# An encoder block's last stage: one run's weight sums made earlier, output rows read early and written in place, the last row tile in two parts

## The chip, the cores and the metric

The kernel runs on 1 core of one Trainium2 chip. The metric is the device time of one execution in microseconds (us). Three executions of the kernel before took 805.09, 804.85 and 802.40 us, median 804.85 us. The execution that was profiled took 804.06 us.

## The reference

One layer of an encoder: 512 positions, width 1024, all inputs in float32.

```python
h = h + rms_norm(mix_out, norm_mix_post)           # gated MLP and attention branches ahead of this
n2 = rms_norm(h, norm_mlp_pre)
hid = jnp.square(jax.nn.relu(einsum('bsd,df->bsf', n2, w_up)))   # 4096 hidden columns
mlp_out = einsum('bsf,fd->bsd', hid, w_down)                     # 512 x 4096 times 4096 x 1024
h = h + rms_norm(mlp_out, norm_mlp_post)                         # the output
```

Everything in this document happens in the last two lines, the down projection, its norm and the sum with `h` (which the kernel keeps in device memory as `h2d`).

## The kernel before, in words

Float32 products are made from three passes: each operand is split into a high part (ACT copies it into a narrower format, line 79) and the rest (DVE subtracts, line 80), and TensorE (PE) adds high*high, high*rest and rest*high (lines 1041, 1042 and 1043). So no matmul of a block can start before ACT and DVE have split it.

The output of the down projection is four row tiles of 128 rows by two halves of 512 columns, in eight banks of PSUM. `X` are the banks of rows 0 and 1 in the left half, `W` rows 0 and 1 in the right half, `Y` rows 2 and 3 in the left half, `Z` rows 2 and 3 in the right half. 32 tiles of 128 hidden columns are to be summed. The first 8 go in plainly (`plain`, four calls of two tiles). The other 24 go through a scheme that gets by with seven products of half the size where eight would be plain; each product here is a **run** of three chunks (`for c in range(NC)`), each chunk 4 x 2 x 3 = 24 matmuls of 128x512, 72 in a run:

| run | bank | activations | weights |
| --- | --- | --- | --- |
| 1 | Y | a21 | `tsum[c]`: a loaded block plus a second one |
| 2 | X | a11 | `block(c, 0, 0)`, loaded as it is |
| 3 | Y | s2 | `tsum[c]` with a third block added |
| 4 | Z | a11 + s2 | `t1`: two blocks added |
| 5 | W | a12 + s2 | `block(c, 1, 1)`, loaded as it is |
| 6 | Y | a22 | `tsum[c]` with a fourth block added |
| 7 | X | a12 | `block(c, 1, 0)`, loaded as it is |

Sums of weight blocks are not made by an engine but by the transfer: `add_block` (line 1064) has the queue of POOL add 1 MB (or 0.5 MB) from device memory onto a tile that lies in SBUF already. Plain loads go through the queue of SP. Both queues issue in program order: what waits at the head holds back all behind it. The order in the program comes from a list scheduler with a cost model; `issue_after` ties single instructions.

Buffers set the pace of loads. `raw_down` tiles (1 MB, tag `raw`) have two buffers; a split block's high and rest parts (`hl`, half a block each) have five; the pool `n2pool` has eight of 0.5 MB, in which the gain row, three `s2`, `v`, the `t1` tiles of run 4 (two for a chunk), and at the end `o` and `h2` lie.

In run 4 (lines 1137 to 1145) each half of a chunk is a `t1` tile of its own: SP loads it (line 1142), POOL's queue adds the second block, ACT and DVE split it. Run 5's blocks come through `raw_down`.

The end: `weigh` (line 1152) squares and sums a row's half on ACT (line 1153) and multiplies it by the gain on DVE (line 1154). `finish` (line 1156) does that for the left half of a row tile, forms the scale (DVE lines 90 and 93, then POOL's power, line 96), loads the tile's rows of `h2d` through POOL's queue (line 1161), forms `o = part * scale + h2` in two halves on DVE (line 1163) and stores them through SP and ACT (line 1165). The right halves are weighed earlier. Runs 6 and 7 go tile by tile in their last chunk, so that the first of two row tiles is finished while the second is still being multiplied.

Of the kernel before, what the change touches and what calls it, by code (L numbers as in the profile page):

```python
# [36 lines left out]
def block_kernel(ctx: ExitStack, tc: tile.TileContext, x, norm_mix_pre, w_in, b_gate, ln_v_gain, ln_v_bias,  # L37
# [50 lines left out]
    def rstd_of(ss, mult, eps=EPS):  # L88
        t = small.tile([P, 1], F32, name="rs_in")
        nc.vector.tensor_scalar(t, ss[:, 0:1], mult, eps, op0=ALU.mult, op1=ALU.add)  # L90
        if ss.shape[1] == 2:
# [1 line left out]
            nc.vector.scalar_tensor_tensor(t2, ss[:, 1:2], mult, t, op0=ALU.mult, op1=ALU.add)
# [2 lines left out]
        nc.gpsimd.tensor_tensor(r, t, neghalf[:, :1], op=ALU.pow)
        return r
# [1053 lines left out]

    def weigh(src, y, junk, ss, hf):
        nc.scalar.activation(junk, src, AF.Square, accum_out=ss[:, 1 - hf:2 - hf])
        nc.vector.tensor_tensor(y, src, gain[:, halves[hf]], op=ALU.mult)

    def finish(t, src, y, early, ss):
        o = n2pool.tile([P, D], F32, name="o", tag="n2")
        weigh(src, y, o[:, halves[0]], ss, 0)
        r = rstd_of(ss, 1.0 / D)
        h2 = n2pool.tile([P, D], F32, name="h2", tag="n2")  # L1160
        nc.gpsimd.dma_start(h2, h2d[tsl[t]])
        for hs, part in zip(halves, (y, early)):
            nc.vector.scalar_tensor_tensor(o[:, hs], part, r, h2[:, hs], op0=ALU.mult, op1=ALU.add)
        for hs, eng in zip(halves, (nc.sync, nc.scalar)):
            eng.dma_start(out[tsl[t], hs], o[:, hs])
# [8 lines left out]

    for c in range(NC):
        for t in chunk(Y, h_split(a22[c]), w_split(tsum[c]), c == NC - 1, c == NC - 1):
            if t is not None:
# [1 line left out]
                finish(2 + t, p1[:, t], p1[:, t], r22[:, t], sums[2 + t])
    for c in range(NC):  # L1180
        for t in chunk(X, h_split(a12[c]), w_split(block(c, 1, 0)), c == NC - 1, c == NC - 1):
            if t is not None:
                finish(t, X[t], lpool.tile([P, 512], F32, name="y"), r12[:, t], sums[t])
# [43 lines left out]
```

## Time and profile before

| | us |
| --- | --- |
| median of three executions | 804.85 |
| profiled execution | 804.06 |
| its span, first to last instruction | 802.3 |
| PE busy | 781.8 |
| DVE busy | 587.2 |
| ACT busy | 452.3 |
| POOL busy | 75.8 |
| last matmul of run 3 starts | 715.95 |
| first matmul of run 4 starts | 719.27 |
| last matmul of run 7 starts | 793.63 |

All starts are counted from the start of the span. What lies outside the span in the profiled execution is 804.06 - 802.3 = 1.76 us. A row of a timeline reads: start, duration, engine, line, operation, output and inputs by their names in the program (`hl`: a split weight block, `hhl`: a split activation block, `pd`: the PSUM banks, `hid`: the four tiles p1, r22, r12 and z0 as well as the hidden columns, `t`: a `t1` tile, `dnw`: a `raw_down` tile, `h`: an `h2` tile), shape, and in brackets the idle time ahead of it with what ended it. Matmuls overlap: the distance between two starts counts, not the duration.

### The profile page before, as it was taken

The page shows a single profiled execution, that of the slowest core. Times are in us where ns is not written, and L with a number is a line of the kernel's source. Part 1 is how long each engine was busy: PE and PEld are TensorE (multiplying, and loading weights), DVE is VectorE, ACT ScalarE, POOL GpSimd, SP SyncE. Part 2 cuts the span into 40 slices and gives each one's busy share as a digit, 9 for nine tenths or more (in the row PEclk, how much of TensorE's full clock was granted, in tenths as well). Part 3 has the DMA queues.
Part 4 walks back from the last instruction along what each step waited for, and adds up shares of the span by engine and source line. Part 5 has one row for each costly group of instructions (what it writes and reads, how often), then busy time and mean ns, then how long its engine had stood idle before and what let it go on. Part 6 is the DMA issues. An engine that isn't in the chain of part 4 may idle for free.

```text
span 802.3 us, 12254 instructions
## 1 busy us (share of the span) xinstructions
PE 781.8 (97%) x4845; PEld 708.1 (88%) x4845; DVE 587.2 (73%) x954; ACT 452.3 (56%) x740; POOL 75.8 (9%) x100
## 2 busy tenths in 40 slices
PE   9999999999999999999999999999999999978995
PEld 6899999999988889999988899899999888856884
DVE  6784689978664877778656489898887645864984
ACT  6351467978586454554445466666666436633670
POOL 2300100010104300000001100000000101122001
PEclk9999999999999999999999999999999999998998
DMA  9733733353626433353446223333334897797514
GB/s 311 231 107 108 206 105 106 91 147 87 173 84 151 125 79 107 98 139 79 146 170 210 79 79 106 106 106 105 106 117 144 281 253 155 246 194 184 184 53 157
DMA packets 101691, 114.65 MB, mean 143 GB/s; under 512 B 3025, under 2 KB 74737, under 8 KB 101634
## 3 DMA queue, kind: packets, MB, share of 16 engines
q1 hardware_dynamic: 84336, 79.70, 32.0%
q0 software_dynamic: 16720, 33.12, 17.1%
q10 hardware_dynamic: 578, 1.05, 0.3%
q8 instruction: 38, 0.62, 0.3%
q14 instruction: 19, 0.16, 0.1%
HBM read 103.90 MB, written 9.96 MB: 142 GB/s over the span
## 4 chain that ended last, share of the span: by engine, by line
PE 91%; DMA 3%; ACT 2%; DVE 2%; issue 1%; POOLq 0%; DVEq 0%; POOL 0%
PE pacc L974 10%; PE pg L343 9%; PE pd L1042 6%; PE pd L1041 6%; PE pd L1043 6%; PE pgacc L343 6%; PE pf L84 5%; PE pf L85 5%; PE pf L86 5%; PE ptp L974 4%; PE pv L84 4%; PE pv L86 4%; PE pv L85 4%; PE pgS L343 3%; PE pd L85 2%; PE pd L84 2%
## 5 line engine op out<-in xcount | busy, mean ns | idle before, releaser
L1042 PE MATMUL pd<-hl,hhl 128*128 128x512 f32 x232 | 91.8, 396 | 3.1 <-DVE hl L80 3.1
L1041 PE MATMUL pd<-hl,hhl 128*128 128x512 f32 x232 | 90.3, 397 | 4.6 <-ACT hl L79 4.6
L1043 PE MATMUL pd<-hl,hhl 128*128 128x512 f32 x232 | 90.2, 394 | 0.0
L974 PE MATMUL pacc<-nt,hl 128*128 128x256 f32 x504 | 67.0, 279 | 1.5 <-DVE u L996 1.5
L974 PEld LDWEIGHTS pacc<-nt,hl 128*128 128x128 f32 x504 | 62.4, 188 | 1.7 <-ACT hid L1012 1.7
L1041 PEld LDWEIGHTS pd<-hl,hhl 128*128 128x128 f32 x232 | 44.1, 191 | 14.5 <-ACT hl L79 5.5
L1042 PEld LDWEIGHTS pd<-hl,hhl 128*128 128x128 f32 x232 | 44.4, 192 | 13.4 <-DVE hl L80 4.2
L1043 PEld LDWEIGHTS pd<-hl,hhl 128*128 128x128 f32 x232 | 44.3, 191 | 9.4
L74 ACT ACTIVATE hi<-s 128x1024 fp32r<-128x1024 f32 x30 | 31.7, 1059 | 24.2 <-DVE s L330 10.8
L974 PE MATMUL pacc<-n,hl 128*128 128x256 f32 x336 | 45.0, 279 | 0.0
L84 PE MATMUL pf<-nh,hi 128*128 128x512 f32 x112 | 44.5, 397 | 0.0
L85 PE MATMUL pf<-nl,hi 128*128 128x512 f32 x112 | 43.9, 392 | 0.0
L86 PE MATMUL pf<-nh,lo 128*128 128x512 f32 x112 | 43.9, 392 | 0.0
L75 DVE TENSOR_TENSOR lo<-s,hi 128x1024 fp32r<-128x1024 f32 x30 | 36.6, 1223 | 9.7 <-ACT hi L74 9.6
L79 ACT ACTIVATE hl<-s 128x1024 fp32r<-128x1024 f32 x28 | 29.4, 1057 | 24.4 <-DVE s L958 14.9
L974 PEld LDWEIGHTS pacc<-n,hl 128*128 128x128 f32 x336 | 41.8, 188 | 0.1
L80 DVE TENSOR_TENSOR hl<-s,hl 128x1024 fp32r<-128x1024 f32 x28 | 34.2, 1220 | 5.8 <-ACT hl L79 5.7
L85 PE MATMUL pv<-lo,nh 128*128 128x512 f32 x96 | 38.2, 397 | 0.0
L80 DVE TENSOR_TENSOR hhl<-hid,hhl 128x1024 fp32r<-128x1024 f32 x19 | 23.1, 1222 | 20.2 <-ACT hhl L79 20.2
L86 PE MATMUL pv<-hi,nl 128*128 128x512 f32 x96 | 37.6, 396 | 0.0
L84 PE MATMUL pv<-hi,nh 128*128 128x512 f32 x96 | 37.6, 398 | 0.0
L79 ACT ACTIVATE hl<-dnw 128x1024 fp32r<-128x1024 f32 x26 | 27.0, 1053 | 17.9 <-PE pacc L974 8.3
(383 smaller groups left out, 2255.8 us busy)
## 6 DMA issues: line engine op xcount, KB each, us to landing
upw<-in_w_up_dram SPq DMA_DIRECT2D x16, 1024.0 KB, 5.5
dnw<-in_w_down_dram SPq DMA_DIRECT2D x13, 1024.0 KB, 5.0
qkw<-in_w_in_dram SPq DMA_DIRECT2D x24, 512.0 KB, 5.2
tsum<-in_w_down_dram POOLq DMA_DIRECT2D x9, 1024.0 KB, 8.6
gw<-in_w_in_dram SPq DMA_DIRECT2D x16, 512.0 KB, 5.3
slab<-in_w_in_dram SPq DMA_DIRECT2D x6, 1024.0 KB, 10.1
wow<-in_w_out_dram SPq DMA_DIRECT2D x4, 1024.0 KB, 5.0
tsum<-in_w_down_dram SPq DMA_DIRECT2D x3, 1024.0 KB, 7.9
```

The lines of the kernel that those rows point to most:

```text
L74: nc.scalar.activation(hi, raw, AF.Copy)
L75: (sub or nc.vector).tensor_tensor(lo, raw, hi.bitcast(F32), op=ALU.subtract)
L79: nc.scalar.activation(hi, src, AF.Copy)
L80: return sub.tensor_tensor(lo, src, hi.bitcast(F32), op=ALU.subtract)
L84: nc.tensor.matmul(ps, ah, bh, start=start, stop=False)
L85: nc.tensor.matmul(ps, ah, bl, start=False, stop=False)
L86: return nc.tensor.matmul(ps, al, bh, start=False, stop=stop)
L343: nc.tensor.matmul(ps, a[:, j], b[:, j], start=first and not (j or i), stop=(j == KH - 1 and i == 2), skip_group_check=True)
L974: nc.tensor.matmul(ps, a[:, j], b[:, j], start=first and not (j or m), stop=(j == KH - 1 and m == 2), skip_group_check=True)
L1041: nc.tensor.matmul(ps, ah, bh, start=start, stop=False, skip_group_check=True)
L1042: nc.tensor.matmul(ps, ah, bl, start=False, stop=False, skip_group_check=True)
L1043: return nc.tensor.matmul(ps, al, bh, start=False, stop=stop, skip_group_check=True)
```

## The change

Four edits, all behind the plain part:

- Run 4's sums. The two tiles of chunk 0 (`near`) are taken from `n2pool`, loaded and summed ahead of run 1. Chunks 1 and 2 are loaded whole into `raw_down` tiles ahead of run 3's loop in the source, that is, behind run 2's three blocks in the rotation of the two buffers, and summed there. Run 5's blocks take the two buffers after them.
- `h2`. All four row tiles are loaded ahead of the last sums through SP (`rows`), into four tiles of `n2pool`, and no longer through POOL one at a time. The tile `o` goes away: the output is formed in place in `rows[t]`, and stored through SP, but for one half of row tile 1.
- `weighed` forms the scale ahead of the product with the gain.
- Row tile 1 of run 7's last chunk is multiplied in two parts of 256 columns, each squared and weighed by itself; its sum of squares has three parts. `issue_after` puts the first part's weighing behind row tile 0's right output half, and row tile 0's left half behind that.

```diff
-        if ss.shape[1] == 2:
+        for k in range(1, ss.shape[1]):
...
+    def t1_sum(c, dst, js=slice(0, 4)):
+        nc.sync.dma_start(dst, w7[c, 0, :, js, halves[0]])
+        add_block(dst, c, 0, 1, js)
+
+    near = [n2pool.tile([P, 2, 512], F32, name="t1", tag="n2") for i in range(2)]
+    for i in range(2):
+        t1_sum(0, near[i], slice(2 * i, 2 * i + 2))
     for c in range(NC):
         run(Y, h_split(a21[c]), w_split(tsum[c]), c == NC - 1)
         add_block(tsum[c], c, 0, 0)
...
+    for c in range(1, NC):
+        t1[c] = raw_down().rearrange("p a (b d) -> p (a b) d", d=512)
+        t1_sum(c, t1[c])
     for c in range(NC):
         run(Y, h_split(s2[c]), w_split(tsum[c]), c == NC - 1)
...
     for c in range(NC):
-        w = []
-        for i in range(2):
-            js = slice(2 * i, 2 * i + 2)
-            t1 = n2pool.tile([P, 2, 512], F32, name="t1", tag="n2")
-            nc.sync.dma_start(t1, w7[c, 0, :, js, halves[0]])
-            add_block(t1, c, 0, 1, js)
-            w.append(split_back(t1, [2, 512]))
+        w = w_split(t1[c]) if c else [split_back(t, [2, 512]) for t in near]
         run(Z, h_split(a11[c]), w, c == NC - 1)
...
+    rows = [n2pool.tile([P, D], F32, name="h2", tag="n2") for _ in range(4)]
+    for t in (2, 3, 0, 1):
+        nc.sync.dma_start(rows[t], h2d[tsl[t]])
...
+    def weighed(t, src, y, k, cols):
+        nc.scalar.activation(v[:, 0, cols], src[:, cols], AF.Square, accum_out=sums[t][:, k:k + 1])
+        r = rstd_of(sums[t], 1.0 / D) if k == sums[t].shape[1] - 1 else None
+        return r, nc.vector.tensor_tensor(y[:, cols], src[:, cols], gain[:, cols], op=ALU.mult)
+
+    def row_out(t, r, part, hf, eng=nc.sync):
+        o = rows[t][:, halves[hf]]
+        ins = nc.vector.scalar_tensor_tensor(o, part, r, o, op0=ALU.mult, op1=ALU.add)
+        eng.dma_start(out[tsl[t], halves[hf]], o)
+        return ins
...
+    for t, cols in ((0, halves[0]), (1, quarter[0]), (1, quarter[1])):
+        with tc.issue_after(final.ins) if final else nullcontext():
+            for j in range(4):
+                wh, wl = w[j // 2]
+                final = acc3(X[t][:, cols], (hh[:, j, tsl[t]], hl[:, j, tsl[t]]), (wh[:, j % 2, cols], wl[:, j % 2, cols]), False, j == 3)
+        if t == 0:
+            r, _ = weighed(0, X[0], y[0], 1, cols)
+            turn = row_out(0, r, r12[:, 0], 1)
+        elif cols == quarter[0]:
+            with tc.issue_after(turn.ins):
+                _, turn = weighed(1, X[1], y[1], 1, cols)
+            with tc.issue_after(turn.ins):
+                row_out(0, r, y[0], 0)
+        else:
+            r, _ = weighed(1, X[1], y[1], 2, cols)
+            row_out(1, r, r12[:, 1], 1, nc.scalar)
+            row_out(1, r, y[1], 0)
```

Three places where instructions move. First POOL's queue from the first `tsum` sum on, before (`tsum` are the sums for runs 1, 3 and 6, three each in this order; the rows with `t_` are run 4's six half sums):

```order
L1064 DMA tsum<-in_w_down_dram 128x4x512 x9
L1064 DMA t_7477<-in_w_down_dram 128x2x512
L1064 DMA t_7483<-in_w_down_dram 128x2x512
L1064 DMA t_7516<-in_w_down_dram 128x2x512
L1064 DMA t_7522<-in_w_down_dram 128x2x512
L1064 DMA t_7555<-in_w_down_dram 128x2x512
L1064 DMA t_7561<-in_w_down_dram 128x2x512
```

and with the change (`t_` is now chunk 0 alone, `dnw` are chunks 1 and 2):

```order
L1064 DMA tsum<-in_w_down_dram 128x4x512 x3
L1064 DMA t_7155<-in_w_down_dram 128x2x512
L1064 DMA t_7156<-in_w_down_dram 128x2x512
L1064 DMA tsum<-in_w_down_dram 128x4x512 x3
L1064 DMA dnw<-in_w_down_dram 128x4x512
L1064 DMA tsum<-in_w_down_dram 128x4x512
L1064 DMA dnw<-in_w_down_dram 128x4x512
L1064 DMA tsum<-in_w_down_dram 128x4x512 x2
```

All of run 4's sums stood behind the ninth `tsum` sum; now chunk 0's stand behind the third, chunk 1's behind the sixth and chunk 2's behind the seventh.

Second, SP's queue behind the last plain block, with the change (lines 1060 are runs 2, 5 and 7, lines 1121 are run 4; before, it read five of line 1060, the six halves of run 4, and four of line 1060):

```order
L1121 DMA t_7155<-in_w_down_dram 128x2x512
L1121 DMA t_7156<-in_w_down_dram 128x2x512
L1060 DMA dnw<-in_w_down_dram 128x4x512 x3
L1121 DMA dnw<-in_w_down_dram 128x4x512 x2
L1163 DMA h_7698<-h2d 128x1024
L1060 DMA dnw<-in_w_down_dram 128x4x512
L1163 DMA h_7699<-h2d 128x1024
L1163 DMA h_7696<-h2d 128x1024
L1060 DMA dnw<-in_w_down_dram 128x4x512
L1163 DMA h_7697<-h2d 128x1024
L1060 DMA dnw<-in_w_down_dram 128x4x512 x4
```

Two of run 5's blocks used to follow run 2's at once; now run 4's chunks 1 and 2 have that place, and all of run 5's come after, with the rows of `h2d` between them.

Third, DVE at the end of run 7, from row tile 0's weighing on, before (what stands in brackets is the engine or queue whose signal the instruction waits for):

```order
L1154 TENSOR_TENSOR y<-pd,gain_6886 128x512 [waits Activation_49]
L93 SCALAR_TENSOR_TENSOR rs_in_7950<-ss_7702,rs_in 128x1
L1154 TENSOR_TENSOR y<-pd,gain_6886 128x512 [waits Activation_49]
L1163 SCALAR_TENSOR_TENSOR o<-y,rs_out,h_7954 128x512 [waits DMASW6_49,Pool_49]
L1163 SCALAR_TENSOR_TENSOR o<-hid,rs_out,h_7954 128x512
L93 SCALAR_TENSOR_TENSOR rs_in_7978<-ss_7703,rs_in 128x1
L1163 SCALAR_TENSOR_TENSOR o<-y,rs_out,h_7982 128x512 [waits DMASW7_49,Pool_49]
L1163 SCALAR_TENSOR_TENSOR o<-hid,rs_out,h_7982 128x512
```

and with the change:

```order
L93 SCALAR_TENSOR_TENSOR rs_in_7945<-ss_7704,rs_in 128x1 [waits Activation_49]
L1175 TENSOR_TENSOR y<-pd,gain_6886 128x512
L1179 SCALAR_TENSOR_TENSOR h_7696<-hid,rs_out,h_7696 128x512 [waits DMAHW7_49,Pool_49]
L1175 TENSOR_TENSOR y<-pd,gain_6886 128x256 [waits Activation_49]
L1179 SCALAR_TENSOR_TENSOR h_7696<-y,rs_out,h_7696 128x512 [waits DVE_49]
L93 SCALAR_TENSOR_TENSOR rs_in_7983<-ss_7705,rs_in 128x1
L93 SCALAR_TENSOR_TENSOR rs_in_7985<-ss_7705,rs_in_7983 128x1 [waits DVE_49,Activation_49]
L1175 TENSOR_TENSOR y<-pd,gain_6886 128x256
L1179 SCALAR_TENSOR_TENSOR h_7697<-hid,rs_out,h_7697 128x512 [waits DMAHW1_49,Pool_49]
L1179 SCALAR_TENSOR_TENSOR h_7697<-y,rs_out,h_7697 128x512 [waits DVE_49]
```

Row tile 1's scale (its last `rs_in`) stood behind both output halves of row tile 0 and is now behind one of them and the weighing of its own first part. On PE, the second part of row tile 1 begins with a wait for DVE; the boundary between the two parts reads:

```order
L1043 MATMUL pd<-hl,hhl 128x256
L1041 MATMUL pd<-hl,hhl 128x256
L1042 MATMUL pd<-hl,hhl 128x256
L1043 MATMUL pd<-hl,hhl 128x256
L1041 MATMUL pd<-hl,hhl 128x256 [waits DVE_49]
L1042 MATMUL pd<-hl,hhl 128x256
L1043 MATMUL pd<-hl,hhl 128x256
```

Before, PE had no wait between its last 24 matmuls but those for the split blocks.

More of the change, by code (lines that the diff above doesn't have):

```diff
@@ L90, in rstd_of @@
         nc.vector.tensor_scalar(t, ss[:, 0:1], mult, eps, op0=ALU.mult, op1=ALU.add)
-        if ss.shape[1] == 2:
+        for k in range(1, ss.shape[1]):
             t2 = small.tile([P, 1], F32, name="rs_in2")
-            nc.vector.scalar_tensor_tensor(t2, ss[:, 1:2], mult, t, op0=ALU.mult, op1=ALU.add)
+            nc.vector.scalar_tensor_tensor(t2, ss[:, k:k + 1], mult, t, op0=ALU.mult, op1=ALU.add)
             t = t2
@@ L1150, in block_kernel @@
         run(W, h_split(s2[c]), w_split(block(c, 1, 1)), c == NC - 1)
[L1152 to L1165, printed above, removed]
@@ L1167, in block_kernel, with weigh @@
-    sums = [small.tile([P, 2], F32, name="ss2") for _ in range(4)]
+    def weigh(src, y, junk, part, cols):
+        nc.scalar.activation(junk, src, AF.Square, accum_out=part)
+        return nc.vector.tensor_tensor(y, src, gain[:, cols], op=ALU.mult)
+    rows = [n2pool.tile([P, D], F32, name="h2", tag="n2") for _ in range(4)]
+    for t in (2, 3, 0, 1):
+        nc.sync.dma_start(rows[t], h2d[tsl[t]])
+    sums = [small.tile([P, 3 if t == 1 else 2], F32, name="ss2") for t in range(4)]
     for i in range(2):
@@ L1169, in block_kernel @@
         nc.vector.tensor_tensor(r22[:, i], Z[i], r22[:, i], op=ALU.add)
-        weigh(r22[:, i], r22[:, i], v[:, i], sums[2 + i], 1)
+        weigh(r22[:, i], r22[:, i], v[:, i], sums[2 + i][:, :1], halves[1])
         nc.vector.tensor_tensor(r12[:, i], Z[i], r12[:, i], op=ALU.add)
         nc.vector.tensor_tensor(r12[:, i], W[i], r12[:, i], op=ALU.add)
-        weigh(r12[:, i], r12[:, i], z0[:, i], sums[i], 1)
+        weigh(r12[:, i], r12[:, i], z0[:, i], sums[i][:, :1], halves[1])
+    def weighed(t, src, y, k, cols):
+        nc.scalar.activation(v[:, 0, cols], src[:, cols], AF.Square, accum_out=sums[t][:, k:k + 1])
+        r = rstd_of(sums[t], 1.0 / D) if k == sums[t].shape[1] - 1 else None
+        return r, nc.vector.tensor_tensor(y[:, cols], src[:, cols], gain[:, cols], op=ALU.mult)
@@ L1178, in block_kernel @@
                 nc.vector.tensor_tensor(p1[:, t], Y[t], p1[:, t], op=ALU.add)
[L1179 to L1183, printed above, removed]
+                r, _ = weighed(2 + t, p1[:, t], p1[:, t], 1, halves[0])
+                row_out(2 + t, r, r22[:, t], 1)
+                row_out(2 + t, r, p1[:, t], 0)
+    for c in range(NC - 1):
+        run(X, h_split(a12[c]), w_split(block(c, 1, 0)), False)
+    (hh, hl), w = h_split(a12[NC - 1]), w_split(block(NC - 1, 1, 0))
+    final = None
+    y = [lpool.tile([P, 512], F32, name="y") for _ in range(2)]
+    quarter = [slice(0, 256), slice(256, 512)]
+    for t, cols in ((0, halves[0]), (1, quarter[0]), (1, quarter[1])):
[15 more added lines that the diff above has]
+            row_out(1, r, y[1], 0)
     dn.close()
```

2 lines of the change are left out of this document (1 added, 1 removed).

## The prediction

> **What bounds the kernel now.** I read the busy times first (PE leads, 781.8 of 802.3 us), then the windows of the last seven runs, then PE's timeline around the only stretch in which it is not busy, then POOL's. The windows (columns: length, busy time and instructions of PE, weight loads, DVE, ACT and POOL, granted PE clock, DMA share, GB/s) are runs 1 to 3, run 4 with its delay, and runs 5 to 7:
>
> ```profile
> 667.20:716.20 49.00, 49.00 (x217) 40.37 (x215) 35.43 (x32) 24.71 (x25) 8.75 (x7) 1.00 0.91 212
> 716.20:745.00 28.80, 21.10 (x74) 15.86 (x74) 18.14 (x17) 13.20 (x13) 4.71 (x5) 0.82 0.82 191
> 745.00:794.10 49.10, 49.02 (x217) 40.27 (x215) 38.04 (x49) 25.64 (x36) 3.96 (x5) 1.00 0.32 115
> ```
>
> Three full runs take 49.0 us, 16.33 each. Run 4 takes 28.8, at a granted clock of 0.82, with as much work. PE there:
>
> ```profile
> 715.95 0.39 PE L1043 MATMUL pd<-hl,hhl 128*128 128x512 f32 x1
> 719.27 1.09 PE L1041 MATMUL pd<-hl,hhl 128*128 128x512 f32 x2 [2.93 <-ACT hl L79]
> 722.93 0.80 PE L1042 MATMUL pd<-hl,hhl 128*128 128x512 f32 x1 [2.57 <-DVE hl L80]
> ...
> 724.80 0.63 PE L1041 MATMUL pd<-hl,hhl 128*128 128x512 f32 x1
> 725.23 0.63 PE L1042 MATMUL pd<-hl,hhl 128*128 128x512 f32 x1
> ...
> 734.18 0.74 PE L1041 MATMUL pd<-hl,hhl 128*128 128x512 f32 x2 [1.68 <-ACT hl L79]
> 735.44 0.50 PE L1042 MATMUL pd<-hl,hhl 128*128 128x512 f32 x1 [0.52 <-DVE hl L80]
> ...
> 793.63 0.39 PE L1043 MATMUL pd<-hl,hhl 128*128 128x512 f32 x1
> ```
>
> It idles 7.7 us in four gaps, and after them starts a matmul every 0.43 us where 0.227 is usual (49.0 us / 216 matmuls). Each gap ends with a split block, and the splits waited for sums:
>
> ```profile
> 706.44 1.29 POOL L1064 DMA_DIRECT2D tsum<-in_w_down_dram  x1 [4.42 <-DVE hl L80]
> 707.18 4.21 POOL L1064 DMA_DIRECT2D t<-in_w_down_dram  x3
> 726.83 1.20 POOL L1064 DMA_DIRECT2D t<-in_w_down_dram  x1 [15.44 <-DMA t<-in_w_down_dram]
> ```
>
> The adds for run 4 start 9 us before the run, behind the last `tsum` add, and only three of the six; the fourth is issued at 726.8, when a buffer has come free and been loaded.
>
> What it costs: run 3's last matmul starts at 715.95, so run 4 could start at 716.18; the work of runs 4 to 7 ends at 793.63 + 0.23 = 793.86. That is 77.68 us for 288 matmuls, which need 288 x 0.2267 = 65.29. **Lost: 12.4 us**, idle and slow clock together.
>
> **Part 1, run 4's sums.** For the whole 12.4 us to go, each block must be summed 2.3 us (one split on ACT, 1.06, and one on DVE, 1.22) before PE's turn, which without gaps comes at 716.2, 721.6 and 727.1 (chunks of 5.44 us): by 713.9, 719.3 and 724.8. The durations of transfers (KB each, us from issue to landing; the windows in which they were issued are named behind):
>
> ```profile
> dnw<-in_w_down_dram SPq DMA_DIRECT2D x2, 1024.0 KB, 5.1
> dnw<-in_w_down_dram SPq DMA_DIRECT2D x1, 1024.0 KB, 17.6
> tsum<-in_w_down_dram POOLq DMA_DIRECT2D x1, 1024.0 KB, 12.7
> tsum<-in_w_down_dram POOLq DMA_DIRECT2D x1, 1024.0 KB, 22.1
> ...
> 682.81 1.21 DVE L80 TENSOR_TENSOR hl<-dnw,hl 128x1024 fp32r<-128x1024 f32 x1
> ...
> 688.73 1.22 DVE L80 TENSOR_TENSOR hl<-dnw,hl 128x1024 fp32r<-128x1024 f32 x1
> ...
> 695.20 1.27 POOL L1064 DMA_DIRECT2D tsum<-in_w_down_dram  x1 [21.19 <-DVE hl L80]
> ```
>
> A plain 1 MB takes 5.1 us (674 to 686) and at the most crowded time 17.6 (643 to 650); an add beside loads 12.7 (630 to 633), and the last of three queued adds 22.1 (636 to 640).
>
> Chunk 1's buffer comes free when run 2's second block is split, 682.81 + 1.21 = 684.0; loaded at 689.1; added beside chunk 2's load, 12.7, by 701.8: 17 us early. Chunk 2's buffer is free at 689.95, loaded at 695.1. Its add is behind the `tsum` add of 695.20 on POOL, so it is issued at 696.5 and lands by 709 at 12.7, by 718.6 at 22.1: 6 us early at worst.
>
> Chunk 0 is loaded and added among the plain part's transfers. There the DMA engines are full, and later not:
>
> ```profile
> 620.00:625.00 5.00, 5.00 (x36) 4.60 (x35) 1.19 (x1) 1.27 (x2) 0.00 (x0) 1.00 0.61 219
> ...
> 630.00:660.00 30.00, 30.00 (x137) 24.91 (x136) 21.12 (x19) 13.85 (x14) 5.17 (x4) 1.00 1.09 280
> 660.00:690.00 30.00, 30.00 (x134) 24.86 (x133) 18.70 (x16) 18.62 (x22) 2.53 (x2) 1.00 0.73 166
> ...
> 732.00:734.00 2.00, 0.51 (x3) 0.09 (x1) 0.14 (x1) 0.93 (x1) 0.21 (x1) 1.00 1.10 201
> ```
>
> Loads alone move 219 / 0.61 = 359 GB/s of a full share, 2.9 us for 1 MB (1.05 million bytes); adds alone 201, 5.2 us. Chunk 0 needs 8.1 us, and from 660 to 690 the engines have 30 x 0.27 = 8.1 us free: by 690 its load and adds, and whatever they push back, are made good. It is wanted at 713.9. What stands behind it on POOL are run 3's adds:
>
> ```profile
> 653.71 1.26 POOL L1064 DMA_DIRECT2D tsum<-in_w_down_dram  x1 [15.99 <-DVE hl L80]
> ...
> 690.15 1.04 ACT L79 ACTIVATE hl<-tsum 128x1024 fp32r<-128x1024 f32 x1
> ```
>
> The first is issued at 653.7, lands by 666.4 at 12.7 and is split at 690.15: 24 us of cover. The last plain block is ahead of chunk 0 on SP. I take 0 for these; with the cover gone each microsecond late would cost one.
>
> The price is run 5. Its first two blocks lay ready before; now the first is loaded when chunk 1 is split. Splits run two blocks ahead of PE because five `hl` buffers let them (the second half of chunk 1 takes the buffer that run 3's last chunk frees half way, at 716.2 - 2.7 = 713.5), so that is done at about 715.7. Chunk 2's comes behind `v` on DVE:
>
> ```profile
> 715.70 1.37 DVE L1135 TENSOR_TENSOR v<-pd,hid 128x512 f32<-128x512 f32 x2 [2.44 <-PE pd L1043]
> ```
>
> From 716.2 on that is 1.37, then six operations of 128x1024 at 1.14 to 1.22 (two subtractions of `v`, a third one, three splits), so it is done at about 724.0. At 5.1 us the blocks land at 720.8 and 729.1, wanted at 732.5 - 2.3 = 730.2 and 735.6. At 17.6 us they land at 733.3 and 741.6 and run 5 loses 3.1 and then 2.9 us: that end is a rival below. I take 5.1, since from 716 on the old run 4 adds no longer occupy the engines. **Part 1: -12.4, at worst -6.4.**
>
> **Part 2, rows of `h2d`.** Four loads of 0.5 MB (1.5 us of the engines each) leave POOL for SP, between run 5's blocks. The first three wait for buffers long free by then, the fourth for the split of the first `s2` of run 5, at about 725; behind it is run 5's third block, not wanted before 741. Cost 0. In-place output has the same eight operations as before. What the earlier load removes from the end is seen in the rows of part 3: nothing, since the last two outputs waited for POOL's power.
>
> **Part 3, the last row tile.** The end before, and behind it four rows for the prices: twelve matmuls of 128x256 in the chain of waits, a 128x256 operation on ACT and on DVE, and POOL's powers (min/median/max in ns):
>
> ```profile
> 791.14 0.39 PE L1041 MATMUL pd<-hl,hhl 128*128 128x512 f32 x1
> ...
> 792.06 0.69 DVE L1154 TENSOR_TENSOR y<-pd,gain 128x512 f32<-128x512 f32 x1 [5.37 <-ACT o L1153]
> 794.55 0.19 ACT L1153 ACTIVATION_READ_ACCUMULATOR o<-pd 128x1 f32 x1
> 794.78 0.69 DVE L1154 TENSOR_TENSOR y<-pd,gain 128x512 f32<-128x512 f32 x1 [1.96 <-ACT o L1153]
> 796.71 0.15 DVE L93 SCALAR_TENSOR_TENSOR rs_in<-ss,rs_in 128x1 f32<-128x1 f32 x1
> 797.02 0.56 POOL L96 TENSOR_TENSOR rs_out<-rs_in,neghalf 128x1 f32<-128x1 f32 x1 [2.95 <-DVE rs_in L93]
> 797.62 0.75 DVE L1163 SCALAR_TENSOR_TENSOR o<-y,rs_out,h 128x512 f32<-128x512 f32 x1 [0.76 <-POOL rs_out L96]
> 798.29 0.75 DVE L1163 SCALAR_TENSOR_TENSOR o<-hid,rs_out,h 128x512 f32<-128x512 f32 x1
> ...
> 629.24 1.40 PE pacc L974 x12
> L995 ACT ACTIVATE p<-ptp 128x256 f32<-128x256 f32 x14 | 5.3, 376 | 6.0 <-PE ptp L974 5.3
> L996 DVE TENSOR_TENSOR u<-pacc,p 128x256 f32<-128x256 f32 x14 | 5.8, 417 | 0.0
> L96 POOL TENSOR_TENSOR rs_out<-rs_in,neghalf x20: 543/563/1407, 5.6 to 797.0; 128x1 f32<-128x1 f32 x20
> ```
>
> Row tile 1's scale waits (794.74 to 796.71) behind row tile 0's two outputs. Now, on this clock: row tile 1 starts at 791.14; twelve matmuls of 128x256 take 1.40, so the first part is done at 792.70. Row tile 0's scale goes first on DVE, 792.06; its power runs 792.36 to 792.92; its right output on DVE 792.96 to 793.70. Only then is the first part weighed, 793.62 to 794.04 (0.42). PE's second part waits for that and starts at 794.08, not at 792.54: **a new gap of 1.5 us**. Behind that wait stand only PE's last twelve matmuls, and for them wait ACT's last square and with it all of row tile 1's output. The second part ends at 795.64; square (0.38) and its sum are ready at 796.13, the scale at 796.32, the power at 797.03, the two outputs at 797.81 and 798.48. Before, the last output ended at 799.04, and from there the stores to the end of the span are the same. **Part 3: -0.55.** Bounds: with the slowest power (1.41 where 0.56 is the median) for both row tiles, +1.1; with no wait on PE the second part ends 1.54 earlier, -2.1.
>
> The Trainium skill, page "PSUM — Partial Sum Buffer", section "PSUM bank collisions raise a hardware error", has software keep two engines apart on one bank and quadrant of partitions whatever the columns, because the chip does not make one wait. By that rule the wait between the two parts can't be spared, and the sum is -0.55 and not -2.1. The row at 794.78, DVE waiting for ACT's read of one bank that both only read, agrees that the program is built so; what the chip does without the wait no run here shows.
>
> **Sum.** Span 802.3 - 12.4 - 0.55 = 789.35; with 1.76 outside the span 791.1 us. The profiled run (804.06) lies 0.8 under the median and 1.7 above the fastest of the three shown: a median of 789.5 to 792 would say the same as 791.1.
>
> **Rivals.**
> - Run 5's blocks land late, at 17.6: +6.0, 797.1 us. For it: a DMA share of 0.91 over runs 1 to 3 before. Against: the load of 17.6 ran in the stretch with a share of 1.09; from 716 only the last `tsum` adds are left beside run 5's blocks.
> - PE isn't held between the two parts: 789.5 us. Against: the wait in PE's order and the row at 794.78.
> - The stall moves whole: chunk 2's add, in one queue with three `tsum` adds, lands so late that run 4 waits as before. From 684 to 716 two loads, one row tile and five adds want 5.8 + 1.5 + 26 = 33.3 us of the engines in 32. Each microsecond past 724.8 costs 12.4 / 7.7 = 1.6 with the slow clock. At 732.5 it lands as late as to cost 12.4: 803.5 us, no change.
> - The other side is the same mechanism from 735.4 on: 10.6 x 1.6 = 17.0 us lost, 808.1 us, slower. That is 39 us after its issue, where 22.1 is the slowest row; nearly excluded.
>
> **How the numbers follow.** Forecast 0.73, run 5 late 0.13, PE not held 0.06, stall moved 0.04, slower 0.04. The first three are faster by over 0.5% (4 us, about what a measurement can tell from no change): 0.92; 0.04 within; 0.04 slower. The range reaches from 788.3 (PE not held, and 1.2 less, as the fastest of the runs shown is 1.7 under the profiled one) to 797 (run 5 late) and leaves the last two out.
>
> **What would show it.** Right: one window from 716 to 782 with PE busy throughout at clock 1.00; `t` and `dnw` adds issued at 640 to 650, 690 and 697; a gap of about 1.5 us on PE ahead of its last 12 matmuls, ended by DVE's `y`; the last output on DVE starting 2.4 us after the last matmul (797.74 - 795.36) where it was 4.7 (798.29 - 793.63). Wrong: ACT waiting for `dnw` between 716 and 750, SP's line 1060 waiting for DVE past 724, or ACT idle on a DMA in the plain part, 630 to 667.

## The result, and the profile after

| | before | after |
| --- | --- | --- |
| median, us | 804.97 (4 runs, 802.40 to 805.86) | 791.61 (4 runs, 791.02 to 792.13) |
| ratio, 95% interval | | 0.9839 [0.9815, 0.9863] |
| profiled execution | 804.06 | 791.23 |
| its span | 802.3 | 789.3 |
| PE busy | 781.8 (97%) | 777.8 (99%) |

The forecast was 791.1 us and a span of 789.35. Medians and ranges in this document leave out three slow executions (1299.87 us of the kernel before, 1567.58 and 1569.00 us in two of the experiments). The windows of after, cut where run 3 ended before and where run 5 begins now (columns as in the prediction: length, busy time of PE, weight loads, DVE, ACT and POOL, granted clock, DMA share, GB/s):

```profile
660.00:690.00 30.00, 30.00 (x134) 24.87 (x133) 18.20 (x16) 19.09 (x23) 2.54 (x2) 1.00 1.00 223
...
667.20:716.20 49.00, 49.00 (x218) 40.59 (x217) 40.34 (x37) 28.80 (x30) 7.69 (x6) 1.00 0.99 217
716.20:732.60 16.40, 16.40 (x74) 13.61 (x73) 12.05 (x11) 7.47 (x8) 0.00 (x0) 1.00 1.06 317
732.60:778.70 46.10, 46.10 (x207) 38.26 (x206) 37.99 (x47) 26.07 (x36) 2.88 (x2) 1.00 0.30 109
```

Run 4 takes 16.4 us where it took 28.8, at a clock of 1.00 where 0.82 was granted: both parts of the loss, the idle time and the slow clock, are gone. The DMA share from 660 to 690 rose from 0.73 to 1.00. That fits chunk 0's load and adds, which go into the free time that the prediction worked out by pushing back what stands behind them: run 3's first add takes 19.2 us to land where it took 11.7. POOL's timeline of after shows the adds of run 4, chunk 0's two halves and then chunks 1 and 2:

```profile
644.90 1.16 POOL L1064 DMA_DIRECT2D t<-in_w_down_dram  x1 [7.89 <-DMA t<-in_w_down_dram]
648.95 1.19 POOL L1064 DMA_DIRECT2D t<-in_w_down_dram  x1 [2.89 <-DMA t<-in_w_down_dram]
...
690.58 1.27 POOL L1064 DMA_DIRECT2D dnw<-in_w_down_dram  x1 [17.02 <-issue]
...
696.50 1.85 POOL L1064 DMA_DIRECT2D dnw<-in_w_down_dram  x1
```

The transfers of after, asked for in short windows (KB each, us to landing): the add of chunk 1, the add of chunk 2, and run 5's first block, which SP issued at 715.6:

```profile
dnw<-in_w_down_dram POOLq DMA_DIRECT2D x1, 1024.0 KB, 12.1
dnw<-in_w_down_dram POOLq DMA_DIRECT2D x1, 1024.0 KB, 16.4
dnw<-in_w_down_dram SPq DMA_DIRECT2D x1, 1024.0 KB, 11.1
```

So chunk 1 is summed at 690.6 + 12.1 = 702.7 and chunk 2 at 696.5 + 16.4 = 712.9, 11.9 us ahead of the 724.8 at which it is wanted. The wait has moved to run 5, in ACT's timeline of after:

```profile
726.69 2.01 ACT L79 ACTIVATE hl<-dnw 128x1024 fp32r<-128x1024 f32 x2 [4.26 <-DMA dnw<-in_w_down_dram]
731.95 2.01 ACT L79 ACTIVATE hl<-dnw 128x1024 fp32r<-128x1024 f32 x2 [2.31 <-DMA dnw<-in_w_down_dram]
```

ACT waits for both of run 5's first blocks, but they land 3.5 and 3.6 us before the times wanted (730.2 and 735.6), and PE has no gap there. The only gap on PE behind run 3 is the new one at the end. PE's timeline of after, the first matmul of row tile 1, the last of its first part, the first and the last of its second part, and under it DVE's:

```profile
778.28 0.28 PE L1041 MATMUL pd<-hl,hhl 128*128 128x256 f32 x1
779.60 0.28 PE L1043 MATMUL pd<-hl,hhl 128*128 128x256 f32 x1
781.29 0.39 PE L1041 MATMUL pd<-hl,hhl 128*128 128x256 f32 x1 [1.42 <-DVE y L1175]
...
782.71 0.28 PE L1043 MATMUL pd<-hl,hhl 128*128 128x256 f32 x1
...
780.15 0.75 DVE L1179 SCALAR_TENSOR_TENSOR h<-hid,rs_out,h 128x512 f32<-128x512 f32 x1
780.82 0.42 DVE L1175 TENSOR_TENSOR y<-pd,gain 128x256 f32<-128x256 f32 x1
...
785.09 0.75 DVE L1179 SCALAR_TENSOR_TENSOR h<-y,rs_out,h 128x512 f32<-128x512 f32 x1
```

The gap of 1.42 us is ended by DVE's `y`, which stands behind row tile 0's right output. The last output starts 785.09 - 782.71 = 2.38 us after the last matmul, where it was 4.66 before (798.29 - 793.63).

### The profile page after: what moved, and what is told of

The parts are those of the page before. It is cut to its first block, busy times and chain, and to the rows that moved or that the text cites. A ratio compares the mean times of both kernels' runs of the same rounds, so it can differ in the third digit from the quotient of the medians.

```text
span 789.3 us, 12279 instructions
## 1 busy us (share of the span) xinstructions
PE 777.8 (99%) x4857; PEld 707.5 (90%) x4857; DVE 586.5 (74%) x956; ACT 451.9 (57%) x742; POOL 71.9 (9%) x94
## 4 chain that ended last, share of the span: by engine, by line
PE 94%; ACT 2%; DMA 1%; DVE 1%; issue 0%; DVEq 0%; POOLq 0%; POOL 0%; ACTq 0%
PE pacc L974 10%; PE pg L343 9%; PE pd L1041 7%; PE pd L1042 7%; PE pd L1043 7%; PE pgacc L343 6%; PE pf L84 5%; PE pf L85 5%; PE pf L86 5%; PE ptp L974 4%; PE pv L84 4%; PE pv L86 4%; PE pv L85 4%; PE pgS L343 3%; PE pd L86 2%; PE pd L84 2%
## 5 line engine op out<-in xcount | busy, mean ns | idle before, releaser
L1041 PE MATMUL pd<-hl,hhl 128*128 128x512 f32 (+1 forms) x236 | 90.6, 386 | 1.4 <-DVE y L1175 1.4
L1042 PE MATMUL pd<-hl,hhl 128*128 128x512 f32 (+1 forms) x236 | 91.1, 386 | 0.0
L1043 PE MATMUL pd<-hl,hhl 128*128 128x512 f32 (+1 forms) x236 | 89.7, 386 | 0.0
L79 ACT ACTIVATE hl<-dnw 128x1024 fp32r<-128x1024 f32 x30 | 31.2, 1055 | 28.5 <-DMA dnw<-in_w_down_dram 11.1
L80 DVE TENSOR_TENSOR hl<-dnw,hl 128x1024 fp32r<-128x1024 f32 x30 | 36.2, 1222 | 11.3 <-ACT hl L79 11.3
## 6 DMA issues: line engine op xcount, KB each, us to landing
tsum<-in_w_down_dram POOLq DMA_DIRECT2D x9, 1024.0 KB, 18.3
```

Source lines behind the costliest of these rows:

```text
L79: nc.scalar.activation(hi, src, AF.Copy)
L80: return sub.tensor_tensor(lo, src, hi.bitcast(F32), op=ALU.subtract)
L1041: nc.tensor.matmul(ps, ah, bh, start=start, stop=False, skip_group_check=True)
L1042: nc.tensor.matmul(ps, ah, bl, start=False, stop=False, skip_group_check=True)
L1043: return nc.tensor.matmul(ps, al, bh, start=False, stop=stop, skip_group_check=True)
```

## The experiments

Eleven runs follow, each timed in three to ten executions beside executions of the kernel before on its own chip (medians 802.9 to 804.0 us). The profiled executions differ by up to 2.5 us in the time at which the down projection begins, and every edit is behind that in the source; so at the end I compare distances from the last matmul and not clock times. For whole kernels I also give, under the name **distance**, the time from the first matmul of the down projection (at 617.99 before, 617.57 after) to the end of the span: 802.3 - 617.99 = 184.31 us before, 171.73 after. It is read from one execution of each kernel, and leaves out what differs ahead of that matmul.

**The change once more.** No edit.

> The changed kernel once more, beside the next three on the same chip. 791.6 us again, span 789.3; PE's gap of 1.4 us ahead of its last twelve matmuls.

790.62 us (790.32 to 791.98), ratio 0.9833 [0.9813, 0.9854], span 790.1, distance 171.82. It is the yardstick of the next three, which ran beside it.

**The sums alone.** The kernel before with only run 4's sums changed:

```diff
+    near = [n2pool.tile([P, 2, 512], F32, name="t1", tag="n2") for i in range(2)]
+    for i in range(2):
+        t1_sum(0, near[i], slice(2 * i, 2 * i + 2))
...
+    for c in range(1, NC):
+        t1[c] = raw_down().rearrange("p a (b d) -> p (a b) d", d=512)
+        t1_sum(c, t1[c])
```

> The kernel before with run 4's sums as in the change (chunk 0 early in n2pool, chunks 1 and 2 in raw_down tiles) and the old ending. My theory: the sums are 12.4 of the 13.0 us of span, so span 789.9, 792.2 us. Rival, that the new ending carries a good part of the gain (a row tile's scale no longer behind two outputs, no loads on POOL): span above 791, time 793 or more.

791.68 us (791.11 to 792.20), ratio 0.9846 [0.9825, 0.9866], span 789.6, distance 172.43. The window of run 4 and the last output, DVE's, behind PE's last matmul:

```profile
716.20:732.60 16.40, 16.40 (x75) 13.55 (x74) 13.48 (x13) 9.07 (x10) 0.56 (x1) 1.00 0.94 286
...
780.42 0.39 PE L1043 MATMUL pd<-hl,hhl 128*128 128x512 f32 x1
...
785.08 0.75 DVE L1168 SCALAR_TENSOR_TENSOR o<-hid,rs_out,h 128x512 f32<-128x512 f32 x1
```

The kernel before had 804.0 us on this chip, so the sums carry 12.3 of the 13.4 us of the whole change. The rest of it is worth 1.06 us by the medians and 0.6 to 0.7 by the distances (172.43 against 171.82 and 171.73). The two spans (790.1 and 789.6) do not show it, because the down projection began 1.1 us earlier in the profiled execution of the sums alone.

**The last row tile undivided.** The change, with row tile 1 multiplied and weighed whole, behind row tile 0's outputs:

```diff
-    for t, cols in ((0, halves[0]), (1, quarter[0]), (1, quarter[1])):
+    for t in range(2):
...
-        elif cols == quarter[0]:
-            with tc.issue_after(turn.ins):
-                _, turn = weighed(1, X[1], y[1], 1, cols)
```

> The changed kernel with row tile 1 of run 7's last chunk multiplied whole again (twelve matmuls of 128x512, one square, one product with the gain), all else as in the change; row tile 0's two outputs stand ahead of row tile 1's weighing on DVE. My theory: the wait on PE that the parts bring costs more than the parts save. Worked out on the trace after: row tile 1 begins at 778.28, its square runs from 781.2, the sum is ready at 781.9, the scale at 782.1, the power at 782.8, the outputs at 783.6 and 784.3, where they were at 785.84: span 787.8, 790.1 us. Rival, that the parts pay: span 789.3 or more, since the last square and product are twice as long.

789.18 us (788.86 to 790.41), ratio 0.9818 [0.9799, 0.9836], span 787.1, distance 169.97. Its end, on PE, DVE, POOL and DVE again:

```profile
780.34 0.39 PE L1043 MATMUL pd<-hl,hhl 128*128 128x512 f32 x1
...
781.55 0.16 DVE L93 SCALAR_TENSOR_TENSOR rs_in<-ss,rs_in 128x1 f32<-128x1 f32 x1 [0.35 <-ACT v L1173]
...
781.86 0.55 POOL L96 TENSOR_TENSOR rs_out<-rs_in,neghalf 128x1 f32<-128x1 f32 x1 [2.17 <-DVE rs_in L93]
...
783.11 0.75 DVE L1179 SCALAR_TENSOR_TENSOR h<-y,rs_out,h 128x512 f32<-128x512 f32 x1
```

The last output starts 2.77 us after the last matmul, 0.39 later than with the two parts, but PE has no gap of 1.42. The two parts cost more than they save: 1.4 us by the medians, 1.8 by the distances.

**No wait between the parts.** The first part is weighed from row tile 0's bank, so that PE's second part has nothing to wait for (the numbers that come out for those columns are other ones):

```diff
-                _, turn = weighed(1, X[1], y[1], 1, cols)
+                _, turn = weighed(1, X[0], y[1], 1, cols)
```

> The changed kernel with one thing else: the first part of row tile 1 is squared and multiplied by the gain from the bank of row tile 0 and not from its own (the left half of that row tile's left output half is computed from other data), so that PE need not wait between the parts. My theory: the gap goes, PE's last matmul starts 1.5 us earlier, at 781.2, and as DVE is then the next to hold things up, the outputs end 1.25 us earlier: span 788.05, 790.3 us. Rival, that PE waits for something else there: a gap of 1 us or more stays and the span is 789.3.

789.50 us (789.17 to 792.57), ratio 0.9827 [0.9805, 0.9850], span 787.2, distance 170.50. The last matmul, on PE without a gap, then on DVE the second part's product with the gain, the last step of row tile 1's scale, and the last output:

```profile
780.20 0.28 PE L1043 MATMUL pd<-hl,hhl 128*128 128x256 f32 x1
...
781.05 0.42 DVE L1175 TENSOR_TENSOR y<-pd,gain 128x256 f32<-128x256 f32 x1
781.38 0.15 DVE L93 SCALAR_TENSOR_TENSOR rs_in<-ss,rs_in 128x1 f32<-128x1 f32 x1
...
782.93 0.74 DVE L1179 SCALAR_TENSOR_TENSOR h<-y,rs_out,h 128x512 f32<-128x512 f32 x1
```

So the wait costs 1.1 us by the medians, 1.2 to 1.3 by the distances. And without it the output starts 2.73 us after the last matmul, as with the whole tile (2.77): the smaller last square is 0.2 us shorter on ACT, and the scale then waits as long for DVE. DVE has row tile 0's left output until 781.06, and in this program it then takes the second part's product with the gain (781.05) ahead of the scale (781.38), where the change has the scale first (783.53 and 783.61). In this order the division gains nothing even where it is free of its wait. With the scale first, the output would come up to 0.3 us earlier, an estimate from the two starts, 781.38 - 781.05; no run shows that.

**The end alone.** The new end with run 4's sums as they were before (the first hunks of the diff undone).

> The kernel before with the new ending alone (rows of h2d through SP, output in place, scale ahead of the product, last row tile in two parts), run 4's sums as before. My theory: -0.5 us of the span, 801.8, 804.2 us, run 4 with its 28.8 us as before, the gap of 1.4 us on PE at the end. Rival, that SP's row loads, which now wait for run 4's tiles ahead of run 5's third block, hold run 5 back: 805 to 808.

805.30 us (803.83 to 807.44), ratio 1.0024 [1.0013, 1.0035], span 803.7: 2 us slower by the medians (805.30 against 803.17) where 0.5 faster was expected. Its transfers issued from 730 to 740, then the last half of chunk 2 on ACT, then PE:

```profile
h<-h2d SPq DMA_DIRECT2D x3, 512.0 KB, 6.2
t<-in_w_down_dram POOLq DMA_DIRECT2D x2, 512.0 KB, 8.4
...
742.38 1.06 ACT L79 ACTIVATE hl<-t 128x1024 fp32r<-128x1024 f32 x1 [5.09 <-DMA t<-in_w_down_dram]
...
743.49 0.73 PE L1041 MATMUL pd<-hl,hhl 128*128 128x512 f32 x2 [2.21 <-ACT hl L79]
...
797.50 0.28 PE L1043 MATMUL pd<-hl,hhl 128*128 128x256 f32 x1
```

The number is the rival's, the cause is not: behind 744.44 PE has no gap until the one between the two parts, so run 5 is not held back. The rows of `h2d` are loaded while run 4's last two adds are under way. Before, the last half was split at 738.43 and PE did not wait for it; now it is split at 742.38 and PE waits 2.21 us. The last matmul starts at 797.50 where it was 793.63. Of these 3.87 us, 0.66 lie ahead of the down projection (run 3's last matmul starts at 716.61 and not at 715.95), 1.42 are the wait between the parts, and some 1.8 are run 4. The shorter tail (799.88 - 797.50 = 2.38) gives back 2.28. I take it from this that part 2 is without cost in the change because run 4's adds are done by then.

**Chunk 0 loaded early, but added late.** In the change, chunk 0's two adds are put behind run 3's last `tsum` add on POOL, and the rows of `h2d` behind run 5's blocks on SP:

```diff
-        t1_sum(0, near[i], slice(2 * i, 2 * i + 2))
+        nc.sync.dma_start(near[i], w7[0, 0, :, 2 * i:2 * i + 2, halves[0]])
...
+    with tc.issue_after(behind.ins):
+        for i in range(2):
+            add_block(near[i], 0, 0, 1, slice(2 * i, 2 * i + 2))
```

> The changed kernel with one order changed: chunk 0 of run 4 is loaded as early as in the change, but its two adds stand on POOL behind run 3's last add, where run 4's adds stood before; the rows of h2d are loaded behind run 5's blocks, so that SP is not held up by chunk 0's tiles. My theory, that the place in POOL's queue and not the load is what made run 4 late: the adds are issued at 707.3 and land at 722 to 725, run 4's first matmul starts at about 724.3 instead of 716.2, with the slow clock about 10 us lost: 798 to 805 us. Rival, that the late loads or the buffers were the cause: 791 us.

803.05 us (802.06 to 804.30), ratio 0.9996 [0.9984, 1.0009]: the whole gain is gone. POOL's two adds, the transfer of both (median us to landing), ACT's split and PE:

```profile
707.43 2.96 POOL L1064 DMA_DIRECT2D t<-in_w_down_dram  x2
...
t<-in_w_down_dram POOLq DMA_DIRECT2D x2, 512.0 KB, 18.1
...
724.59 1.06 ACT L79 ACTIVATE hl<-t 128x1024 fp32r<-128x1024 f32 x1 [12.35 <-DMA t<-in_w_down_dram]
...
725.70 1.22 PE L1041 MATMUL pd<-hl,hhl 128*128 128x512 f32 x2 [9.12 <-ACT hl L79]
```

One gap of 9.1 us, and the slow clock behind it (0.69 from 716.2 to 732.6). Two adds of 0.5 MB at the wrong place in one queue, with chunks 1 and 2 summed early, cost as much as all six did before. The early load does nothing by itself; the add's place does it.

**Chunk 0 alone early.** In the change, chunks 1 and 2 are loaded and summed in run 4's loop, as before:

```diff
+            if c:
+                js = slice(2 * i, 2 * i + 2)
+                t = n2pool.tile([P, 2, 512], F32, name="t1", tag="n2")
+                t1_sum(c, t, js)
```

> The changed kernel with chunks 1 and 2 of run 4 as before (half tiles of n2pool, loaded and added behind run 3's adds; run 5's first two blocks lie ready again). My theory: chunk 0 without delay, chunk 1 about on time, chunk 2's last half waits for a buffer that chunk 1 gives back at about 720, is added by 733 where 727.5 is wanted: 6 to 8 us lost with the slow clock, 796 to 800 us. Rival, that the early chunk 0 alone gives POOL and the engines enough room: 792 us or less.

802.47 us (801.01 to 804.54), ratio 0.9989 [0.9976, 1.0003]. Much less was left of the gain than expected. SP's four loads, POOL's last add, ACT's split and PE:

```profile
691.63 33.12 SPq L1121 DMA_DIRECT2D t<-in_w_down_dram  x4
...
730.71 1.20 POOL L1064 DMA_DIRECT2D t<-in_w_down_dram  x1 [7.07 <-DVE hl L80]
...
738.76 1.06 ACT L79 ACTIVATE hl<-t 128x1024 fp32r<-128x1024 f32 x1 [9.55 <-DMA t<-in_w_down_dram]
...
739.87 2.17 PE L1041 MATMUL pd<-hl,hhl 128*128 128x512 f32 x4 [4.75 <-ACT hl L79]
```

Chunk 0 runs without a gap, until 721.85. Then PE waits 2.8 us for chunk 1 and 4.75 for the last half of chunk 2, whose load SP issues only at 691.63 + 33.12 = 724.75 (in SP's order it waits for DVE, whose splits free the buffers of `n2pool`); both waits are followed by the slow clock. The last add is issued at 730.71 where it was 731.01 before, and takes 8.0 us to land where it took 7.3, with the rows of `h2d` loaded beside it from 725.5 on. The gain does not come in thirds: what one chunk wins, the next one loses, because the last add sets the end of run 4. Neither chunk 0 alone nor, in the run before, chunks 1 and 2 alone keep more than 0.7 us of it by the medians; other divisions were not tried.

**The rows ahead of run 5's blocks.** In the change, the four loads of `h2d` stand ahead of run 5's first block on SP.

> The changed kernel with all four row loads ahead of run 5's blocks on SP, so that the fourth, which waits for the split of the first s2 of run 5 (done at 724.8), holds run 5's first block back from 715.55 to about 725.2. This measures how near the change comes to the rival of the late run 5. My theory: run 5's first block had 3.5 us to spare (landed 726.7, wanted 730.2), so it now lands at 731 to 736 and 1 to 6 us are lost: 792.5 to 797 us, with a gap on PE at 732.5. Rival, that the queue holds nothing up because the block's transfer is quicker when it starts later: 791 us.

794.47 us (793.41 to 794.56), ratio 0.9883 [0.9860, 0.9905], span 792.5, distance 175.71: 4.0 us more than in the change. The last three of the four row loads and then the blocks of runs 5 and 7 on SP, ACT's split of run 5's first block, and PE:

```profile
706.64 17.75 SPq L1157 DMA_DIRECT2D h<-h2d  x3
724.44 19.98 SPq L1060 DMA_DIRECT2D dnw<-in_w_down_dram  x5
...
730.36 2.01 ACT L79 ACTIVATE hl<-dnw 128x1024 fp32r<-128x1024 f32 x2 [3.25 <-DMA dnw<-in_w_down_dram]
...
734.48 0.80 PE L1042 MATMUL pd<-hl,hhl 128*128 128x512 f32 x1 [2.28 <-DVE hl L80]
```

The fourth row waits for its buffer, and run 5's first block behind it until 724.4. It lands 3.7 us later than in the change, just past the 3.5 that were to spare, and PE waits 2.28 us, with seven matmuls at half pace behind it. Part of this wait is DVE's: in this program four additions of run 4's result (from 730.81 to 733.2) come ahead of the split, in the change behind it. How much each has of the 4 us was not taken apart.

**The order of the scale alone.** The prediction gave the new end one price. To see which of its edits earns it, the sums alone got the new order on DVE: the scale ahead of the product with the gain, row tile 1's scale behind row tile 0's outputs; `o` and the loads of `h2d` through POOL stay.

```diff
-        weigh(src, y, o[:, halves[0]], ss, 0)
-        r = rstd_of(ss, 1.0 / D)
+        with tc.issue_after(turn.ins) if turn else nullcontext():
+            nc.scalar.activation(o[:, halves[0]], src, AF.Square, accum_out=ss[:, 1:2])
+            r = rstd_of(ss, 1.0 / D)
+        with tc.issue_after(scales[-1].ins):
+            nc.vector.tensor_tensor(y, src, gain[:, halves[0]], op=ALU.mult)
```

> Kernel before with run 4's sums as in the change, and of the new end only the order on DVE: a row tile's scale ahead of its product with the gain, and row tile 1's scale behind row tile 0's outputs as in the version with the undivided tile. Output tile o and the rows of h2d through POOL's queue stay as before. It tells apart what the new end owes to the order and what to the rows that are loaded ahead. Theory A (both count): the scales come as in the undivided version, row tile 1's power ends at 782.4, but its rows of h2d, issued behind row tile 0's power at about 779.7, land 3.5 us later at 783.2, so its outputs start at 783.2 and 783.9 where the undivided version has 782.44 and 783.11: span 787.9, time 789.9. Theory B, that of the prediction's second part (the earlier loads remove nothing): span 787.1, time 789.2. Rival C (the order is worth nothing, the gain of the end is in the rows): as with the sums alone, span 789.6, time 791.7.

792.10 us (791.42 to 793.16), ratio 0.9863 [0.9845, 0.9881], distance 172.06: the order alone gains next to nothing (0.4 by the distances, against 172.43). PE's last matmul, POOL's load of row tile 1's rows, and DVE's last two outputs:

```profile
782.44 0.39 PE L1045 MATMUL pd<-hl,hhl 128*128 128x512 f32 x1
...
781.70 0.58 POOL L1171 DMA_DIRECT2D h<-h2d  x1
...
786.12 0.75 DVE L1173 SCALAR_TENSOR_TENSOR o<-y,rs_out,h 128x512 f32<-128x512 f32 x1 [1.78 <-DMA h<-h2d]
786.79 0.74 DVE L1173 SCALAR_TENSOR_TENSOR o<-hid,rs_out,h 128x512 f32<-128x512 f32 x1
```

The outputs wait 1.78 us for the rows of `h2d`, whose load stands behind row tile 0's power on POOL and takes 4.3 us to land. Theory A had this wait, but at 0.75, from a load of 3.5.

**The undivided tile again**, beside the run before.

> The change with its last row tile undivided once more, beside the run before, so that the two are compared on one chip. Theory A: 789.2, span 787.1, and 0.7 us under the run with the order alone; theory B: equal to it.

788.99 us (788.67 to 790.38), ratio 0.9830 [0.9811, 0.9849], distance 170.18: 3.1 us under the order alone by the medians, 1.9 by the distances. The down projection begins 2.5 us earlier in this profiled execution than in that of the order alone, so part of the 3.1 may lie ahead of it.

**The rows alone.** The sums alone, with the rows loaded ahead through SP and the output formed in them; the scale stays behind the product:

```diff
-        nc.gpsimd.dma_start(h2, h2d[tsl[t]])
...
+    rows = [n2pool.tile([P, D], F32, name="h2", tag="n2") for _ in range(4)]
+    for t in (2, 3, 0, 1):
+        nc.sync.dma_start(rows[t], h2d[tsl[t]])
```

> Kernel before with run 4's sums as in the change, and of the new end only the rows of h2d: loaded ahead through SP into four tiles, the output formed in place in them; the scale stays behind the product with the gain, the last row tile undivided, the stores as before. With the sums alone (791.7), the order alone (792.1) and both (789.1) it fills the fourth place of a table. Theory (rows loaded behind POOL's power were what held the last output, and the order counts only once they are gone): row tile 0's product 778.8 to 779.4, its power to 780.3, its outputs to 781.75; row tile 1's product to 782.4, its power to 783.2, its outputs from 783.26 and 783.93 where the undivided change has 782.44 and 783.11: 0.8 us more than that, span 787.9, 790.0 us. Rival (the rows alone are worth nothing, as the prediction says of them): like the sums alone, last output at 785.1, span 789.6, 791.7 us.

791.16 us (790.85 to 793.32), ratio 0.9853 [0.9834, 0.9873], span 789.1, distance 171.32. Its end, on PE, DVE, POOL and DVE again:

```profile
780.98 0.39 PE L1043 MATMUL pd<-hl,hhl 128*128 128x512 f32 x1
...
781.62 0.74 DVE L1166 SCALAR_TENSOR_TENSOR h<-hid,rs_out,h 128x512 f32<-128x512 f32 x1
782.28 0.68 DVE L1159 TENSOR_TENSOR y<-pd,gain 128x512 f32<-128x512 f32 x1
...
783.18 0.55 POOL L96 TENSOR_TENSOR rs_out<-rs_in,neghalf 128x1 f32<-128x1 f32 x1 [2.26 <-DVE rs_in L93]
...
784.44 0.74 DVE L1166 SCALAR_TENSOR_TENSOR h<-hid,rs_out,h 128x512 f32<-128x512 f32 x1
```

The edit brought an order with it. Row tile 0's outputs (780.95 and 781.62) now stand ahead of row tile 1's product with the gain (782.28) on DVE; in the sums alone they stand behind it (782.18 and 782.84, the product at 781.57), although row tile 0's rows, issued at 770.73, land within 5.0 us and its power ends at 780.32. So row tile 1's scale no longer waits for two outputs behind a product, and what is gained here is not the rows' alone. The order alone has row tile 0's outputs at the earlier place too.

From the last matmul's start to the last output's start, in us, with run 4's sums early and the last tile undivided:

| | rows of `h2d` late, through POOL | rows early, through SP |
| --- | --- | --- |
| scale behind the product | 4.66 (791.68) | 3.46 (791.16) |
| scale ahead of it | 4.35 (792.10) | 2.77 (789.18, 788.99) |

The column of the rows brings 1.2 or 1.6, the order 0.3 or 0.7, both 1.9. Only the 1.6 can be put down to the rows, since the 1.2 holds the new place of row tile 0's outputs; early rows in the old order of DVE were not tried. The medians in brackets (three chips) also carry what differs ahead of the down projection, and do not order the first three; that both edits together are the fastest stands out. By the distances it is 172.43 and 172.06 on the left, 171.32 and 169.97 or 170.18 on the right. There both together gain 0.4 to 0.6 us more, behind the start of the last output, for which I did not look for a cause. The undivided change is the fastest kernel measured, 1.7 to 1.8% under the kernel before.

## Why the prediction was right

- **Part 1, -12.4 of the span.** Right. The sums alone brought 12.3 us of the median, and from the first matmul of the down projection to its last 12.39 (175.64 before, 163.25). The 12.7 by which the span is shorter is in part luck, since 0.8 of it lies ahead of the down projection. The causes are as named: with the adds late again the gain is zero (chunk 0 added late), and PE's idle time and the slow clock come back together. The 0 for chunk 0's place among the plain part's transfers held: PE busy throughout from 630 to 716. Run 3's first add took 19.2 us to land and not the 12.7 of the prediction, which the 24 us of cover had room for.
- **Chunks 1 and 2.** Forecast 701.8 and 709 to 718.6, found 702.7 and 712.9. The rival that the stall moves whole would have needed 732.5.
- **Run 5.** The mechanism was right, a size was off. The step "I take 5.1, since from 716 on the old run 4 adds no longer occupy the engines" failed: the first load was issued when forecast (715.55 for about 715.7) but took 11.1, so that landing was 726.7 and not 720.8, the second 731.95 and not 729.1. The DMA share from 716.2 to 732.6 is 1.06: the last two `tsum` adds, issued at 700.25 and 706.00 and so no later than before, now take 18.3 and 20.1 us where they took 8.1 and 8.4, and land at 718.6 and 726.1. The rows of `h2d` on SP are not the cause, since in the sums alone, where SP has none of them and POOL one row tile's load, the same load takes 10.9. The forecast margin of 9.4 us (730.2 - 720.8) was 3.5; the rows ahead of run 5 used it up, which is in part the rival's way, at 4.0 us for 6.0. Two of the signs that the prediction named for being wrong did show: ACT waits for `dnw` at 726.69 and 731.95, and SP's line 1060 waits for DVE until 730.17. The time came out all the same because 3.5 us were left, and by this sum, with 5.1 for 11.1, that is luck.
- **Part 2, cost 0.** Right in the change, by place: one row tile's load is issued at 691.04, the other three behind run 5's first block. The end alone and the rows ahead of run 5 give it some 1.8 and 4 us at other places.
- **"What the earlier load removes from the end is seen in the rows of part 3: nothing, since the last two outputs waited for POOL's power."** Wrong as a step, for the order on DVE that the change has. The row read did name POOL's power, but the rows of `h2d` landed only some 0.6 us earlier (in the sums alone issued at 780.28, 3.5 us to landing, outputs from 784.41). Two causes stood almost level, and the second showed when the first moved: 1.78 us of waiting in the order alone. The -0.55 did hold the gain of both, since it was worked out from the new order of rows that lay ready.
- **Part 3, -0.55.** The gap (1.54 forecast, 1.42 found) and the tail (2.38 in both) were as worked out. The whole end is worth -1.06 by the medians, -0.6 to -0.7 by the distances, and -0.4 from the first matmul of the down projection to the start of the last output (167.91 in the sums alone, 167.52 after): the term is within what can be told. But it hid a loss: it set the divided tile against the old end and not against the same new end undivided, which is 1.4 us faster. The lower bound of -2.1, PE not held, came out at -2.2 by the medians (789.50 against 791.68 of the sums alone) and at -1.9 by the distances.
- By the rule that the page "PSUM — Partial Sum Buffer" of the Trainium skill gives in its section "PSUM bank collisions raise a hardware error", software has to keep DVE's read of the first part and PE's write of the second part apart, since both lie in one bank: the gap of 1.42 us ended by DVE's `y` shows the program doing it. What the chip would do without it was not tried.

## What to carry to other kernels

A queue that issues in program order makes the place of a transfer, and not the time at which its data are ready, the thing to look at: two adds of 0.5 MB behind the wrong neighbour cost 12 us here, and moving one of three chunks was worth next to nothing. When a wait is named in the profile, look for the cause that stands just behind it, since the gain of removing one of two nearly level causes is small (0.3 us for the order alone) and shows in full only when both go (1.9). When one edit lets the scheduler choose another order, read the order again before putting the gain down to the edit. Before dividing a last tile to shorten a tail, price the wait that the division makes on the engine that sets the end against the undivided tile in the same order.

## What the runs showed of the hardware beyond that

- PE's pace after a gap: behind the wait of 2.21 us in the end alone it went on at full pace (a matmul of 128x512 every 0.23 us), and behind that of 1.42 in the change too (one of 128x256 every 0.12), though only 1.4 us of matmuls were left there. Behind 2.28 in the rows ahead of run 5, and behind 4.75 and 9.12, matmuls started every 0.43 us for 3 to 6 us. In chunk 0 alone early it was half pace behind 2.09 and 0.72 with two matmuls between them. In the kernel before, behind 1.68 and 0.52, full pace came first and half pace only from 736.48 on, with no gap there. So the idle time of one gap does not settle it; what else enters was not looked for.
- An add takes long beside others, and not the same each time: in one execution adds of 1 MB took 12.1 and 16.4 us, and the two adds of 0.5 MB issued together behind a third took 18.1.
- POOL's power took 0.55 us at the end, beside DVE's product of a PSUM bank with the gain (779.34 to 780.02), and 0.88 and 2.00 earlier, beside DVE's products and splits of tiles that lie in SBUF. Whether that is the cause was not tested. The last two of the three, in POOL's timeline of after:

```profile
770.92 2.00 POOL L96 TENSOR_TENSOR rs_out<-rs_in,neghalf 128x1 f32<-128x1 f32 x1 [3.39 <-DVE rs_in L93]
779.57 0.55 POOL L96 TENSOR_TENSOR rs_out<-rs_in,neghalf 128x1 f32<-128x1 f32 x1 [6.65 <-DVE rs_in L93]
```
